# Stick-breaking mixers: which engine makes the weights' low parts and products, and where the values are evacuated

## The chip, the cores and the metric

One core of a Trainium2 chip runs the whole program in one launch. The metric is device microseconds for one execution, the median of the timed runs. Five engines run queues of their own in order: TensorE (PE; its weight loads are shown apart, as PEld), VectorE (DVE), ScalarE (ACT), GpSimd (POOL), and SP, which issues the DMAs. They are tied by semaphores.

## The reference, cut to what matters

The model is one block of dilated attention, SSM and convolution, and behind it two layers of a second kind. Each layer of the second kind is FFN, mixer, FFN, with RMS norms around them. Only the two mixers are touched. x has 512 tokens of 1024 channels; a mixer has 8 heads of 64 channels.

```python
proj = h @ w_in
q, k, v, gate_b, gate_c, conv_h, pool_in = jnp.split(proj, SPLIT_POINTS, axis=-1)
attn = _stick_breaking_attention(q, k, v)
conv = gate_b * causal_conv3(gate_c * conv_h)
pool = _multiscale_pool(pool_in, pool_w, pool_scale)   # trailing means minus the token
return jnp.concatenate([attn, conv, pool], axis=-1) @ w_out

# one query block of stick-breaking attention
z = q_blk @ k.T / sqrt(dh)                             # masked to keys before the query
log_keep = where(mask, log_sigmoid(-z), 0)
between = reverse_cumsum(log_keep) - log_keep
a = where(mask, exp(log_sigmoid(z) + between), 0)      # sigmoid(z) * product of later (1 - sigmoid)
out = a @ v
```

## The kernel before

**Precision and layout.** Channels lie on the partitions (tiles of 128 x 512 tokens). Every product of float32 matrices is made of three passes of rounded numbers: each operand is kept as a high part (ScalarE's cast) and a low part (raw minus high), and `mm3` (lines 111 to 113) multiplies high by high, low by high and high by low.

**Weights.** `Weights.prepare` (line 309 makes the low part) takes the next 512 KB of weights that a DMA has brought, lets ScalarE cast the high part `wh` and another engine subtract the low part `wl`: VectorE when no engine is named, POOL for `prepare(nc.gpsimd)`. Three raw buffers and four pairs of parts rotate.

**A mixer** (`mixer2`) runs over eight heads, n = 0 to 7, and fills TensorE's time between a head's steps with projections ("units"), by the table `FILL`: a unit is 24 matmuls of 512 columns into a bank, then an evacuation on VectorE. The names are q and k (queries and keys of a pair of heads), p (pooling input), m (pooling map, only three matmuls), g, c, l (the three parts of the convolution). Heads 0, 2, 6 and 7 have one long unit, the others two. For head n:

- `scores`: eight matmuls into three PSUM banks z; VectorE adds the mask (line 1670).
- the head before: `turn` transposes its weights (ten matmuls, line 612) into three banks, `rest` takes the low part `tl` on VectorE (line 628); `flush` splits queries into high and low parts (lines 572, 573).
- `weights`: ScalarE makes sigmoid(z) (`pr`) and sigmoid(-z) (`keep`); VectorE scans `keep` along the keys, four scans (line 1686); three products `pr` times shifted `keep` follow on POOL (line 1689).
- the first unit begins, `prepare` runs on POOL, 18 of its 24 matmuls run, then `values` of the head before: eight matmuls into the only bank `av`, and behind them the evacuation at once: ScalarE copies one half (`o`, line 1705), VectorE adds the other (line 1706), ScalarE casts the high part `oh`, VectorE subtracts the low part `ol` (line 103), on the 64 partitions of that head.
- the unit ends; at odd n the key unit's result is scaled on VectorE (`qk`, line 1855) and split at once: ScalarE copies k (lines 581, 583), VectorE makes `kl` (line 582). The scores of head n + 1 need these copies.
- further units of `FILL[n]`, a second `prepare` on POOL, and at some heads the pooling windows and means on POOL (lines 1777 to 1792).

The queues follow the order of this code (a manual schedule): nothing overtakes.

What is quoted below is printed by a program with the line numbers of the profile.

Of the kernel before, what the change touches and what calls it, by code (L numbers as in the profile page):

```python
# [10 lines left out]
ALU = mybir.AluOpType  # L11
AX = mybir.AxisListType

P = 128
# [526 lines left out]
QPLACE = [(1, 384), (2, 0), (1, 0), (0, 0)]  # L541
# [349 lines left out]
class Ssm:  # L891
# [162 lines left out]
    def collect(self, h):  # L1054

        y = self.k.gt("y", F32)
        self.k.nc.vector.scalar_tensor_tensor(y[:, :].rearrange("p (t j) -> p j t", j=L), self.u[h][:, ::-1],
                                              self.vec["dskip"][:, h:h + 1], self.yp.pop(h), ALU.mult, ALU.add)
        self.y.append(y)
# [586 lines left out]
class StickHead(Head):  # L1646
# [25 lines left out]
    def weights(self):  # L1672
        k, nc, zs = self.k, self.k.nc, self.zs
        self.pr, keep = [], []
        for b in range(3):
            w = WIDTH[b]
            p, e = k.gt("pr", F32), k.gt("keep", F32)
            nc.scalar.activation(e[:, :w], zs[b][:, :w], AF.Sigmoid, scale=-1.0)
            nc.scalar.activation(p[:, :w], zs[b][:, :w], AF.Sigmoid)
            self.pr.append(p)  # L1680
            keep.append(e)
        for qb in (3, 2, 0, 1):
            b, c = QPLACE[qb]
            e = keep[b][:, c:c + (qb + 1) * P][:, ::-1]
            zero = k.zero[:, 0:1].to_broadcast([P, (qb + 1) * P])
            nc.vector.tensor_tensor_scan(e, e, zero, 1.0, ALU.mult, ALU.add)  # L1686
        for b in range(3):
            n = WIDTH[b] - 1
            nc.gpsimd.tensor_tensor(self.pr[b][:, :n], self.pr[b][:, :n], keep[b][:, 1:n + 1], ALU.mult)

    def values(self):

        k, rows = self.k, self.rows
        c, n = divmod(self.h, 2)
        cols = slice(c * P, (c + 1) * P)
        av = k.pav.tile([P, S], F32, tag="av", name=k.uid("av"))
        for kb in range(4):
            b, c = KPLACE[kb]
            cs = slice(c, c + S - kb * P)
            for x in (self.th[b], self.tl[b]):  # L1700
                k.nc.tensor.matmul(av[:, kb * P:S], self.v[kb][n][:, cols], x[:, cs],
                                   start=kb == 0 and x is self.th[b], stop=kb == 3 and x is self.tl[b],
                                   skip_group_check=True)
        o = k.tmp("o")
        k.nc.scalar.copy(o[rows], av[self.other])
        k.nc.vector.tensor_tensor(o[rows], av[rows], o[rows], ALU.add)
        k.split(self.oh[rows], self.ol[rows], o[rows])


class Channel:  # L1710
# [23 lines left out]
class ShortConv:  # L1734
# [10 lines left out]
    def do_conv(self, ps):  # L1745
        k, nc, y, cw = self.k, self.k.nc, self.gc, self.cw
        hh = k.tmp("hh")
        nc.vector.tensor_tensor(hh, ps, self.st.R, ALU.mult)
        nc.vector.tensor_tensor(hh, y, hh, ALU.mult)
        nc.scalar.activation(y, hh, AF.Copy, scale=cw(2))  # L1750
        nc.vector.scalar_tensor_tensor(y[:, 1:], hh[:, :S - 1], cw(1), y[:, 1:], ALU.mult, ALU.add)
        nc.vector.scalar_tensor_tensor(y[:, 2:], hh[:, :S - 2], cw(0), y[:, 2:], ALU.mult, ALU.add)
        nc.gpsimd.tensor_tensor(y, y, self.st.R, ALU.mult)

    def do_last(self, ps):
        k = self.k
# [86 lines left out]
def mixer2(k, l, X, st, first, vec, gpost, gnext, start):  # L1843
    nc = k.nc
# [14 lines left out]
    def flush():  # L1859
        while later:  # L1860
            later.pop(0)()
# [4 lines left out]
    def unit(name):  # L1866
        kind, i = name[0], int(name[1])
        if kind in "qk":
            return query_key(i, "qk".index(kind))
        return {"p": lambda: pool[i].input, "m": lambda: pool[i].map, "g": lambda: conv[i].gate,  # L1870
                "c": lambda: conv[i].conv, "l": lambda: conv[i].last}[kind]()
# [11 lines left out]
    flush()  # L1883
    v += [first.end(tt) for tt in range(2, 4)]
    unit("p0").whole()
    prev = None
    for n in range(8):
        if n % 2 == 0:
            slot(n // 2)
        head = StickHead(k, n, qk[n // 2], v, (oh[n // 2], ol[n // 2]))  # L1890
        head.scores()
        if prev:
            prev.turn()
            prev.rest()
            flush()
        head.weights()
        u = unit(FILL[n][0])
        u.begin(False)
        k.w.prepare(nc.gpsimd)
        u.run(0, 6)  # L1900
        if prev:
            prev.values()
        u.run(6, KT)
        u.end()
        if n % 2:
            flush()
        for name in FILL[n][1:]:
            u = unit(name)
            u.begin(False)
            u.run(0, len(u.hi))  # L1910
            u.end()
        k.w.prepare(nc.gpsimd)
        if n % 2 == 0 and n < 4:
            pool[n // 2].windows()
        if n == 0 or n == 3:
            pool[n // 2].mean()
        if n == 1:
            pool[0].prepare()
        if n == 4:
            pool[1].prepare()  # L1920
        prev = head
# [6 lines left out]
    last.end()  # L1928
    flush()
    prev.values()  # L1930


    post = PostNorm(k, X, gpost, gnext)
# [143 lines left out]
```

## Time and profile before

| | us |
|---|---|
| median of three timed runs | 2549.23 |
| lowest and highest | 2548.54, 2550.1 |
| the profiled execution | 2553.54 |
| its span, first to last instruction | 2551.8 |
| TensorE busy in it | 2476.5 |
| VectorE busy | 1262.1 |
| ScalarE busy | 997.5 |
| POOL busy | 586.5 |

The profiled execution is one execution under the profiler, and times of single instructions come from it. A matmul's record is longer than its share of TensorE's time, since matmuls are pipelined: 512 columns stand at 0.39 us, and the next starts about 0.23 us later. "Idle before" an instruction is time in which its engine did nothing, and the arrow names what ended it. An engine's instruction that is blocked inside the engine looks like a long instruction, not like a wait. The first mixer's heads lie between 1046 and 1167 us of the span, the second's between 2002 and 2123.

### The profile page before, as it was taken

The page shows a single profiled execution, that of the slowest core. Times are in us where ns is not written, and L with a number is a line of the kernel's source. Part 1 is how long each engine was busy: PE and PEld are TensorE (multiplying, and loading weights), DVE is VectorE, ACT ScalarE, POOL GpSimd, SP SyncE. Part 2 cuts the span into 40 slices and gives each one's busy share as a digit, 9 for nine tenths or more (in the row PEclk, how much of TensorE's full clock was granted, in tenths as well). Part 3 has the DMA queues.
Part 4 walks back from the last instruction along what each step waited for, and adds up shares of the span by engine and source line. Part 5 has one row for each costly group of instructions (what it writes and reads, how often), then busy time and mean ns, then how long its engine had stood idle before and what let it go on. Part 6 is the DMA issues. An engine that isn't in the chain of part 4 may idle for free.

```text
span 2551.8 us, 30104 instructions
## 1 busy us (share of the span) xinstructions
PE 2476.5 (97%) x11792; PEld 2052.8 (80%) x11792; DVE 1262.1 (49%) x1848; ACT 997.5 (39%) x1576; POOL 586.5 (23%) x556
## 2 busy tenths in 40 slices
PE   8898999999999999999999999999999999999998
PEld 4687888888888888778788888888888778788887
DVE  6657575543534424774633423533424874643422
ACT  3356444332433323654433223433323654433322
POOL 7213220001211102473311101211102473311101
PEclk9999999999999999999999999999999999999999
DMA  6333444332233232212233232233332212223232
GB/s 247 103 123 112 151 155 156 117 99 91 91 99 98 89 96 81 68 59 91 84 98 99 87 100 87 91 99 99 92 92 81 68 59 91 90 92 99 87 102 68
DMA packets 87697, 254.80 MB, mean 100 GB/s; under 512 B 13698, under 2 KB 19842, under 8 KB 87556
## 3 DMA queue, kind: packets, MB, share of 16 engines
q1 hardware_dynamic: 86980, 252.35, 31.1%
q8 instruction: 93, 1.52, 0.2%
q10 hardware_dynamic: 576, 0.52, 0.1%
q14 instruction: 48, 0.39, 0.0%
HBM read 249.56 MB, written 3.39 MB: 99 GB/s over the span
## 4 chain that ended last, share of the span: by engine, by line
PE 80%; DVE 11%; ACT 3%; POOL 2%; issue 2%; DMA 1%; SPq 0%; DVEq 0%; ACTq 0%; POOLq 0%
PE mm L111 25%; PE mm L113 25%; PE mm L112 25%; DVE keep L1686 2%; PE mm L344 2%; DVE wa L507 1%; DVE acc L441 1%; POOL x L1587 1%; DVE fs L1579 1%; DVE x L1587 1%; DVE xl L107 1%; DVE q L573 1%; DMA wa<-wada 1%; PE n L372 1%; DVE tl L628 1%
## 5 line engine op out<-in xcount | busy, mean ns | idle before, releaser
L309 DVE TENSOR_TENSOR wl<-wr,wh 128x1024 fp32r<-128x1024 f32 (+2 forms) x383 | 448.7, 1176 | 936.0 <-ACT wh L308 935.7
L308 ACT CAST wh<-wr 128x1024 fp32r<-128x1024 f32 (+3 forms) x444 | 430.7, 979 | 549.9 <-PE mm L112 510.0
L111 PE MATMUL mm<-xh,wh 128*128 128x512 f32 x1568 | 616.4, 393 | 0.4
L113 PE MATMUL mm<-xh,wl 128*128 128x512 f32 x1568 | 611.5, 390 | 0.0
L112 PE MATMUL mm<-xl,wh 128*128 128x512 f32 x1568 | 611.4, 390 | 0.0
L111 PEld LDWEIGHTS mm<-xh,wh 128*128 128x128 f32 x1568 | 295.3, 188 | 62.5 <-DVE ol L107 1.4
L113 PEld LDWEIGHTS mm<-xh,wl 128*128 128x128 f32 x1568 | 295.0, 188 | 62.3 <-DVE wl L309 0.5
L111 PE MATMUL mm<-gh,wh 128*128 128x512 f32 (+1 forms) x936 | 343.7, 367 | 0.0
L112 PEld LDWEIGHTS mm<-xl,wh 128*128 128x128 f32 x1568 | 295.3, 188 | 60.1
L113 PE MATMUL mm<-gh,wl 128*128 128x512 f32 (+1 forms) x936 | 342.0, 365 | 0.0
L112 PE MATMUL mm<-gl,wh 128*128 128x512 f32 (+1 forms) x936 | 342.0, 365 | 0.0
L1631 POOL TENSOR_TENSOR ff<-ff,R 128x512 f32<-128x512 f32 x88 | 113.7, 1293 | 789.8 <-ACT ff L1630 789.8
L441 POOL TENSOR_TENSOR acc<-acc,sq 128x512 f32<-128x512 f32 (+1 forms) x85 | 93.9, 1104 | 717.3 <-ACT sq L428 716.4
L112 PEld LDWEIGHTS mm<-gl,wh 128*128 128x128 f32 x936 | 176.5, 189 | 28.8
L111 PEld LDWEIGHTS mm<-gh,wh 128*128 128x128 f32 x936 | 176.5, 189 | 28.8
L113 PEld LDWEIGHTS mm<-gh,wl 128*128 128x128 f32 x936 | 176.5, 189 | 28.2
L309 POOL TENSOR_TENSOR wl<-wr,wh 128x1024 fp32r<-128x1024 f32 (+2 forms) x61 | 135.3, 2227 | 243.7 <-ACT wh L308 242.7
L111 PE MATMUL mm<-uh,wh 128*128 128x512 f32 x424 | 170.5, 402 | 6.7 <-DVE vl L103 6.7
L112 PE MATMUL mm<-ul,wh 128*128 128x512 f32 x424 | 166.3, 392 | 0.0
L113 PE MATMUL mm<-uh,wl 128*128 128x512 f32 x424 | 166.2, 392 | 0.0
L102 ACT CAST gh<-ff 128x512 fp32r<-128x512 f32 x88 | 54.7, 621 | 171.1 <-DVE ff L1633 171.1
L1630 ACT ACTIVATE ff<-ff 128x512 f32<-128x512 f32 x88 | 55.6, 632 | 155.9 <-DVE ff L1629 155.8
(350 smaller groups left out, 3258.7 us busy)
## 6 DMA issues: line engine op xcount, KB each, us to landing
wr<-wg SPq DMA_DIRECT2D x88, 512.0 KB, 3.5
wr<-wu SPq DMA_DIRECT2D x88, 512.0 KB, 3.5
wr<-wd SPq DMA_DIRECT2D x80, 512.0 KB, 3.5
wr<-wi SPq DMA_DIRECT2D x56, 512.0 KB, 3.5
wa<-wada SPq DMA_DIRECT2D x64, 256.0 KB, 4.6
wr<-wup SPq DMA_DIRECT2D x32, 512.0 KB, 3.5
wr<-wo SPq DMA_DIRECT2D x24, 512.0 KB, 3.5
wr<-wd SPq DMA_DIRECT2D x32, 384.0 KB, 3.1
```

The source lines that it names most:

```text
L102: self.nc.scalar.copy(hi, raw)
L111: mm(out, wh, xh, start=start, stop=False, **kw)
L112: mm(out, wh, xl, start=False, stop=False, **kw)
L113: mm(out, wl, xh, start=False, stop=stop, **kw)
L308: self.k.nc.scalar.copy(hi[:, a:b], raw[:, a:b])
L309: e.tensor_tensor(lo[:, a:b], raw[:, a:b], hi[:, a:b].bitcast(F32), ALU.subtract)
L344: mm = lambda ps, w, x, a, b: k.nc.tensor.matmul(ps[:, cs], w, x, start=a, stop=b, skip_group_check=True)
L441: engine.tensor_tensor(self.acc[:, c0:c1], self.acc[:, c0:c1], sq[:, c0:c1], ALU.add)
L1587: engine.tensor_tensor(x, x, self.f[i][:, cs], ALU.add)
L1630: nc.scalar.activation(t, t, AF.Silu)
L1631: nc.gpsimd.tensor_tensor(t, t, st.R, ALU.mult)
L1686: nc.vector.tensor_tensor_scan(e, e, zero, 1.0, ALU.mult, ALU.add)
```

## The change

Four things are edited. The low parts of the weights at both places of a head, and the three products of the weights and the convolution's last product (`gc`), are issued on VectorE instead of POOL; each product stands right behind the scans of its bank. `values` ends with its matmuls; the new `collect` evacuates them, and is called behind `flush`, so behind the key's scaling and its copies. Copy and sum of a head still work on its 64 partitions, but both heads of a pair write into one tile `o`, and the split into `oh` and `ol` is made once for the pair, at the odd head, over 128 partitions.

```diff
--- before.py
+++ after.py
@@ -1679,14 +1679,14 @@
             nc.scalar.activation(p[:, :w], zs[b][:, :w], AF.Sigmoid)
             self.pr.append(p)
             keep.append(e)
-        for qb in (3, 2, 0, 1):
-            b, c = QPLACE[qb]
-            e = keep[b][:, c:c + (qb + 1) * P][:, ::-1]
-            zero = k.zero[:, 0:1].to_broadcast([P, (qb + 1) * P])
-            nc.vector.tensor_tensor_scan(e, e, zero, 1.0, ALU.mult, ALU.add)
-        for b in range(3):
+        for b, qbs in enumerate(((3,), (2, 0), (1,))):
+            for qb in qbs:
+                c = QPLACE[qb][1]
+                e = keep[b][:, c:c + (qb + 1) * P][:, ::-1]
+                zero = k.zero[:, 0:1].to_broadcast([P, (qb + 1) * P])
+                nc.vector.tensor_tensor_scan(e, e, zero, 1.0, ALU.mult, ALU.add)
             n = WIDTH[b] - 1
-            nc.gpsimd.tensor_tensor(self.pr[b][:, :n], self.pr[b][:, :n], keep[b][:, 1:n + 1], ALU.mult)
+            nc.vector.tensor_tensor(self.pr[b][:, :n], self.pr[b][:, :n], keep[b][:, 1:n + 1], ALU.mult)
 
     def values(self):
 
@@ -1701,10 +1701,18 @@
                 k.nc.tensor.matmul(av[:, kb * P:S], self.v[kb][n][:, cols], x[:, cs],
                                    start=kb == 0 and x is self.th[b], stop=kb == 3 and x is self.tl[b],
                                    skip_group_check=True)
-        o = k.tmp("o")
+        self.av = av
+
+    def collect(self, pair):
+
+        k, rows, av = self.k, self.rows, self.av
+        if not pair:
+            pair.append(k.tmp("o"))
+        o = pair[0]
         k.nc.scalar.copy(o[rows], av[self.other])
         k.nc.vector.tensor_tensor(o[rows], av[rows], o[rows], ALU.add)
-        k.split(self.oh[rows], self.ol[rows], o[rows])
+        if self.h % 2:
+            k.split(self.oh, self.ol, pair.pop())
 
 
 class Channel:
@@ -1750,7 +1758,7 @@
         nc.scalar.activation(y, hh, AF.Copy, scale=cw(2))
         nc.vector.scalar_tensor_tensor(y[:, 1:], hh[:, :S - 1], cw(1), y[:, 1:], ALU.mult, ALU.add)
         nc.vector.scalar_tensor_tensor(y[:, 2:], hh[:, :S - 2], cw(0), y[:, 2:], ALU.mult, ALU.add)
-        nc.gpsimd.tensor_tensor(y, y, self.st.R, ALU.mult)
+        nc.vector.tensor_tensor(y, y, self.st.R, ALU.mult)
 
     def do_last(self, ps):
         k = self.k
@@ -1883,7 +1891,7 @@
     flush()
     v += [first.end(tt) for tt in range(2, 4)]
     unit("p0").whole()
-    prev = None
+    prev, pair = None, []
     for n in range(8):
         if n % 2 == 0:
             slot(n // 2)
@@ -1896,7 +1904,7 @@
         head.weights()
         u = unit(FILL[n][0])
         u.begin(False)
-        k.w.prepare(nc.gpsimd)
+        k.w.prepare()
         u.run(0, 6)
         if prev:
             prev.values()
@@ -1904,12 +1912,14 @@
         u.end()
         if n % 2:
             flush()
+        if prev:
+            prev.collect(pair)
         for name in FILL[n][1:]:
             u = unit(name)
             u.begin(False)
             u.run(0, len(u.hi))
             u.end()
-        k.w.prepare(nc.gpsimd)
+        k.w.prepare()
         if n % 2 == 0 and n < 4:
             pool[n // 2].windows()
         if n == 0 or n == 3:
@@ -1928,6 +1938,7 @@
     last.end()
     flush()
     prev.values()
+    prev.collect(pair)
 
 
     post = PostNorm(k, X, gpost, gnext)
```

On POOL at the begin of the first mixer, before (`pr`: products of the weights; `wl`: low parts of weights; `s`, `d`: pooling windows and means):

```order
L1689 TENSOR_TENSOR pr_8170<-pr_8170,keep_8171 128x511
L1689 TENSOR_TENSOR pr_8174<-pr_8174,keep_8175 128x511
L1689 TENSOR_TENSOR pr_8178<-pr_8178,keep_8179 128x255
L309 TENSOR_TENSOR wl_8191<-wr_8059,wh_8190 128x1024
L309 TENSOR_TENSOR wl_8223<-wr_8065,wh_8222 128x128
L1777 COPY s_8228<-p_8152 128x1
L1778 TENSOR_TENSOR s_8228<-p_8152 128x511
L1786 COPY d_8231<-s_8228 64x512
L1787 COPY d_8231<-s_8228 64x2
L1788 TENSOR_TENSOR d_8231<-s_8228 64x510
```

and the same place with the change:

```order
L1785 COPY s_8228<-p_8152 128x1
L1786 TENSOR_TENSOR s_8228<-p_8152 128x511
L1794 COPY d_8231<-s_8228 64x512
L1795 COPY d_8231<-s_8228 64x2
L1796 TENSOR_TENSOR d_8231<-s_8228 64x510
L1798 TENSOR_TENSOR d_8231<-d_8231,cst 128x16
L1799 TENSOR_SCALAR d_8231<-d_8231,cst 128x496
L1800 TENSOR_TENSOR d_8231<-d_8231,p_8152 128x512
L1785 COPY s_8505<-p_8375 128x1
L1786 TENSOR_TENSOR s_8505<-p_8375 128x511
```

Products and low parts are gone, and the pooling branch of head 0 (d_8231) and then that of head 2 (from s_8505) stand first on POOL, with nothing ahead of them.

On VectorE, from head 1's scans (`keep`) to the end of its key and value work, before (`o`, `ol`: the values of head 0; `qk`, `kl`: the key; `p`: the pooling input; `dl`: its low part; `z`: masks of head 2):

```order
L1686 SCALAR_TENSOR_TENSOR keep_8284<-keep_8284,zero 128x512
L1686 SCALAR_TENSOR_TENSOR keep_8288<-keep_8288,zero 128x384
L1686 SCALAR_TENSOR_TENSOR keep_8288<-keep_8288,zero 128x128
L1686 SCALAR_TENSOR_TENSOR keep_8292<-keep_8292,zero 128x256
L1706 TENSOR_TENSOR o_8330<-av_8321,o_8330 64x512
L103 TENSOR_TENSOR ol_8155<-o_8330,oh_8154 64x512
L1855 SCALAR_TENSOR_TENSOR qk_8341<-mm_8302,R_6943 128x512
L582 TENSOR_TENSOR kl_8345<-qk_8341,k_8343 64x512
L582 TENSOR_TENSOR kl_8345<-qk_8341,k_8344 64x512
L1770 TENSOR_TENSOR p_8377<-mm_8352,R_6943 128x512
L103 TENSOR_TENSOR dl_8386<-d_8231,dh_8385 128x512
L1670 TENSOR_TENSOR z_8391<-z_8391,cst 128x128
```

and with the change:

```order
L1687 SCALAR_TENSOR_TENSOR keep_8284<-keep_8284,zero 128x512
L1689 TENSOR_TENSOR pr_8283<-pr_8283,keep_8284 128x511
L1687 SCALAR_TENSOR_TENSOR keep_8288<-keep_8288,zero 128x384
L1687 SCALAR_TENSOR_TENSOR keep_8288<-keep_8288,zero 128x128
L1689 TENSOR_TENSOR pr_8287<-pr_8287,keep_8288 128x511
L1687 SCALAR_TENSOR_TENSOR keep_8292<-keep_8292,zero 128x256
L1689 TENSOR_TENSOR pr_8291<-pr_8291,keep_8292 128x255
L1863 SCALAR_TENSOR_TENSOR qk_8336<-mm_8302,R_6943 128x512
L582 TENSOR_TENSOR kl_8340<-qk_8336,k_8338 64x512
L582 TENSOR_TENSOR kl_8340<-qk_8336,k_8339 64x512
L1713 TENSOR_TENSOR o_8347<-av_8321,o_8347 64x512
L1778 TENSOR_TENSOR p_8375<-mm_8350,R_6943 128x512
```

The three products have come between the scans; the key's scaling and low parts have moved ahead of the values' sum; the values' low part is gone here, since head 0 is the first of its pair; a low part of weights follows behind the pooling input.

## Rows read from the trace of the kernel before

**Rows 1.** The page's chain of waits: share of the span by engine

```profile
PE 80%; DVE 11%; ACT 3%; POOL 2%; issue 2%; DMA 1%; SPq 0%; DVEq 0%; ACTq 0%; POOLq 0%
```

**Rows 2.** Windows of both mixers: stretch, length, busy us (count) by engine, clock

```profile
1046.30:1167.00 120.70, 111.13 (x529) 90.56 (x528) 99.72 (x135) 71.16 (x130) 81.86 (x61) 0.97 0.19 62
2002.30:2123.00 120.70, 111.11 (x529) 90.56 (x528) 99.61 (x135) 71.19 (x131) 81.80 (x61) 0.97 0.20 62
```

**Rows 3.** What TensorE waited for, first mixer: total us, times, longest

```profile
PE z L1661 <- ACT k L583: 6.3, 3, 2.4
PE mm L612 <- POOL pr L1689: 1.5, 4, 0.7
```

**Rows 4.** Window after the longest key wait, columns as in rows 2

```profile
1102.10:1109.00 6.90, 6.90 (x23) 5.85 (x23) 5.14 (x9) 5.00 (x11) 5.22 (x5) 0.51 0.28 89
```

**Rows 5.** VectorE's groups, first mixer: busy us, mean ns | idle before

```profile
L1686 DVE TENSOR_TENSOR_SCAN keep<-keep,zero 128x512 f32<-128x512 f32 (+3 forms) x32 | 34.7, 1144 | 0.2
L573 DVE TENSOR_TENSOR q<-qk,q 64x512 fp32r<-64x512 f32 x6 | 8.0, 1331 | 0.2
L103 DVE TENSOR_TENSOR ol<-o,oh 64x512 fp32r<-64x512 f32 x7 | 7.2, 1034 | 5.0 <-ACT oh L102 5.0
L582 DVE TENSOR_TENSOR kl<-qk,k 64x512 fp32r<-64x512 f32 x6 | 4.9, 818 | 3.3 <-ACT k L581 3.2
L103 DVE TENSOR_TENSOR dl<-d,dh 128x512 fp32r<-128x512 f32 x2 | 3.2, 1586 | 0.8 <-ACT dh L102 0.8
L1749 DVE TENSOR_TENSOR hh<-gc,hh 128x512 f32<-128x512 f32 x2 | 2.8, 1424 | 0.1
```

**Rows 6.** VectorE's groups by form, same stretch: the 384-column scan

```profile
L1686 DVE TENSOR_TENSOR_SCAN keep<-keep,zero 128x384 f32<-128x384 f32 x8 | 7.4, 928 | 0.0
```

**Rows 7.** Timeline: POOL, then VectorE's scans: start, us, idle before

```profile
1061.78 1.04 POOL L1788 TENSOR_TENSOR d<-s 64x510 f32<-64x510 f32 x1
...
1065.31 1.29 POOL L1792 TENSOR_TENSOR d<-d,p 128x512 f32<-128x512 f32 x1
1061.80 5.35 DVE L1686 TENSOR_TENSOR_SCAN keep<-keep,zero 128x512 f32<-128x512 f32 x4
```

**Rows 8.** VectorE's groups by form, whole span: prices

```profile
L309 DVE TENSOR_TENSOR wl<-wr,wh 128x1024 fp32r<-128x1024 f32 x319 | 393.2, 1238 | 808.5 <-ACT wh L308 808.3
L103 DVE TENSOR_TENSOR gl<-ff,gh 128x512 fp32r<-128x512 f32 x88 | 61.0, 693 | 60.5 <-ACT gh L102 60.5
...
L628 DVE TENSOR_TENSOR tl<-mm,th 128x256 fp32r<-128x256 f32 x8 | 3.3, 415 | 0.0
```

**Rows 9.** POOL's groups, first mixer, columns as in rows 5

```profile
L309 POOL TENSOR_TENSOR wl<-wr,wh 128x1024 fp32r<-128x1024 f32 (+1 forms) x15 | 34.7, 2325 | 9.9 <-ACT wh L308 9.9
L1689 POOL TENSOR_TENSOR pr<-pr,keep 128x511 f32<-128x511 f32 (+1 forms) x24 | 27.5, 1162 | 35.2 <-DVE keep L1686 35.2
L1753 POOL TENSOR_TENSOR gc<-gc,R 128x512 f32<-128x512 f32 x2 | 2.9, 1456 | 8.8 <-DVE gc L1752 8.8
```

**Rows 10.** VectorE's waits for ScalarE, first mixer, columns as in rows 3

```profile
DVE ol L103 <- ACT oh L102: 5.0, 7, 0.8
DVE kl L582 <- ACT k L581: 3.2, 5, 0.8
DVE gc L1751 <- ACT gc L1750: 1.6, 2, 0.8
DVE o L1706 <- ACT o L1705: 1.6, 2, 1.1
```

**Rows 11.** Timeline at head 1's end: VectorE, then TensorE

```profile
1067.07 0.65 DVE L1706 TENSOR_TENSOR o<-av,o 64x512 f32<-64x512 f32 x1
1069.55 0.67 DVE L1855 SCALAR_TENSOR_TENSOR qk<-mm,R 128x512 f32<-128x512 f32 x1
1071.57 0.91 PE L1661 MATMUL z<-k,q 128*128 128x512 f32 x4 [1.81 <-ACT k L583]
```

**Rows 12.** Window of head 2, columns as in rows 2

```profile
1071.50:1081.50 10.00, 9.93 (x52) 8.44 (x53) 8.55 (x13) 8.30 (x16) 3.46 (x2) 1.00 0.18 54
```


## The prediction

> **What bounds the kernel now.** The chain of waits first: four fifths of the span are TensorE's own matmuls and most of the rest is VectorE [rows 1]. The change touches only the two mixers, so I then read each mixer as one stretch, from the first score matmul to the last values matmul. They are alike: 120.7 us each, VectorE busy for 99.7 us, POOL for 81.9, the granted clock 0.97 on average [rows 2]. TensorE waits there mostly for the keys' copies (6.3 us in three waits, the longest 2.4) and for the product of the weights, which POOL makes (1.5 us) [rows 3]. After the longest of the key waits the clock falls to half (1.2 of 2.4 GHz), 0.51 over 6.9 us [rows 4], which costs about 3.4 us of matmuls. So 11 us of each stretch are TensorE's losses, and VectorE, though not the engine that is fullest, stands in front of nearly all of them. The reader is to see that VectorE's 99.7 us are not all work. A scan of 384 columns takes 0.93 us [rows 6]; the four scans of a head have 1280 columns together, so 3.1 us by the same price, 24.7 us for eight heads, and they took 34.7 [rows 5]. The timeline shows why: beside four POOL instructions that ran one after the other from 1061.78 to 1066.60, the four scans took 5.35 us, and their ends take turns with POOL's [rows 7]. VectorE's instructions with two SBUF operands stand still while a POOL instruction runs.
>
> The Trainium skill says so too (SBUF — State Buffer, section "SBUF: two separate sides"): the pair of ports that VectorE and GpSimd share is locked for a whole instruction and the other engine blocks fully. The trace agrees in kind; how much of POOL's record that is, the rows decide below.
>
> **The change, part by part, for one mixer.** All is summed on VectorE's own time, because after the change it is the engine with the most work that waits for others.
>
> What goes away with POOL's work is the blocking. Against the free price of 0.69 us for 512 columns [rows 8] the groups with two SBUF operands lose: scans 34.7 − 24.7 = 10.0; the query splits 8.0 − 6 × 0.69 = 3.9; the values' low parts 7.2 − 7 × 0.69 = 2.4; the keys' low parts 4.9 − 4.1 = 0.8; the pooling branch's low parts 3.2 − 1.4 = 1.8; the convolution's product 2.8 − 1.4 = 1.4 [rows 5]. Together 20.3 us. VectorE's work as such is 99.7 − 20.3 = 79.4 us.
>
> What comes to VectorE: 24 products of the weights, 16 of 511 columns at 0.69 us and 8 of 255 columns at 0.42 [rows 8], 14.4 us (POOL took 27.5 for them [rows 9]). Fifteen low parts of weights (34.7 us on POOL [rows 9]): thirteen of 128x1024 at 1.24 us [rows 8] less 0.08, because records that follow each other overlap (32 scans of 1.144 cover 34.7 and not 36.6 [rows 5]), 15.1 us, and two of 128x128, at most 0.4 each, 0.8. Two products of the convolution, 1.4 us (2.9 on POOL [rows 9]). The values' low parts are halved, since one instruction over 128 partitions takes as long as one over 64: seven in the stretch become three, −2.8 us. Sum +28.9 us, so 108.3 us.
>
> The GPSIMD Engine Reference of the Trainium skill (section 4.1, "Engine selection") speaks for this part: elementwise work belongs on VectorE, GPSIMD being about twice as slow with two inputs. The rows agree (1.24 against 2.33 us for the weights). By that rule alone the change is a gain; what it would give is the first rival.
>
> What is left of the blocking: POOL keeps the pooling windows and means, 81.9 − 34.7 − 27.5 − 2.9 = 16.8 us [rows 2, 9]. Before, they stood on POOL behind products and low parts; now nothing stands ahead of them, so they start as soon as their input is evacuated, and in heads 0 and 2 they meet the scans and products on VectorE. The bounds are 0 (all of it falls on VectorE's idle time or beside its PSUM readers) and 16.8 (one for one). In the row that is nearest, four scans lost 5.35 − 3.1 = 2.3 us to 4.8 us of POOL [rows 7], which is half, so I take 8.4 us: 116.7.
>
> What is left of VectorE's waits: it answers ScalarE inside one queue, and these replies stay. Keys 3.2, convolution 1.6, values' copy 1.6, and the values' hi part, 5.0 for seven, now 2.1 for three [rows 10]: 8.5 us. Nothing else is queued on VectorE that could run meanwhile. The wait for the transposed weights (th) I leave out, since VectorE will come late there. 116.7 + 8.5 = 125.2 us, against 120.7 now: +4.5 us a mixer, +9.0 for both.
>
> The keys' evacuation is a gain of place, and it is in the sum already. In head 1 the values' sum began at 1067.07 and the key's scaling only at 1069.55, after which TensorE waited 1.81 us for the key [rows 11]. Now the key's scaling stands right behind the third product, and 2.48 us come before it no more, but three products (1.8 us) do: 0.7 us earlier by order, and some 2 us more because the scans are not blocked. So the key waits shrink or go, and with them the drop of the clock. What is late next is the transposes. Each needs the products of the head before and a PSUM bank that VectorE must evacuate behind two low parts of weights. It is worst in the short heads, where TensorE has only one long accumulation: in the stretch of head 2 VectorE is busy 8.55 of 10.0 us already [rows 12], and it gets 1.8 us of products and two low parts of 1.2 us more, against some 3 us that are freed or hidden. So I expect idle time of 2 to 5 us in front of the transposes of heads 0 and 2 and of the last heads, and with idle time in such clusters a clock at half there too. While VectorE sets the pace, a slow clock costs little.
>
> Queues: POOL issues no DMA, and the loads on SP wait for the raw buffers, which are freed when a low part is done; these are done sooner or as soon. ScalarE loses 4 copies of 0.6 us a mixer, hidden. The last values of a mixer are evacuated as before, and the code behind it is the same: 0.
>
> **Which time it is compared with.** The sum was made inside a profiled execution of 2553.54 us (span 2551.8). The three timed runs have a median of 2549.23; I put the difference on that: 2549.2 + 9.0 = 2558.2 us.
>
> **The rivals.** (1) *Faster: VectorE keeps up.* POOL's windows and means fall beside VectorE's idle time and readers of PSUM and block nothing. Then the sum is 108.3 + 8.5 = 116.8 us, −3.9 a mixer, 2541.4 us. For it: the key waits (6.3 us) and the half clock (3.4 us) are the largest losses, and the change goes at just these. Against it: both pooling branches now run exactly beside scans and products. It decides from 3.9 us of blocking a mixer on: below that the kernel is faster than before. (2) *No difference*: blocking of 2 to 6 us; what the keys give, the transposes take: 2545 to 2554 us. (3) *Worse: POOL blocks for its whole record*, 16.8 us: 133.6 us, +12.9 a mixer, 2575 us. For it: a VectorE instruction and a POOL instruction take turns one for one in the rows, and the chain has seven links instead of four. Against it: POOL's records contain its own waiting for the lock. The rule of the Trainium skill on the locked pair (SBUF — State Buffer, "SBUF: two separate sides"), taken at its word, gives this end. (4) *The later evacuation holds the only bank of the values* until the next head's values want it: a wait of under 1 us in one or two heads, inside the range.
>
> **How the numbers follow.** About 0.2% (5 us) can be told from no change. My forecast, VectorE bound with some half of the blocking, 2554.5 to 2568 us: 0.52. Rival 3, above 2568: 0.09. Rival 2: 0.22. Rival 1, below 2544: 0.17. So slower 0.61, same 0.22, faster 0.17. The range of 8 in 10 is 2542 to 2568: it leaves out about 0.1 at each end, and corresponds to 0.3 to 13 us of blocking a mixer.
>
> **What would show it.** Right: VectorE over 95% of the stretch in use or waiting for ScalarE, its scans at 0.4 to 1.25 us outside heads 0 and 2, POOL's windows beside the first head's scans, TensorE's waits for keys down from 6.3 to under 2 us, and new waits of transposes and of their banks for VectorE of over 10 us a mixer, the stretch 122 to 130 us long. Wrong: key waits gone and no new ones for the transposes (rival 1); scans of head 0 over 10 us with their products (rival 3); or a stretch outside the mixers that has changed, which my sum says cannot be.

## The result and the profile after

The changed kernel takes 2564.6 us (median of four runs, 2560.58 to 2566.98) where the kernel before takes 2549.55 on the same chip: a ratio of 1.0057, 95% interval 1.0041 to 1.0073. It is slower by some 15 us. The profiled execution took 2566.98 us, its span is 2565.2 us, 13.4 more than before. The page's chain of waits has moved by one point from TensorE to VectorE [rows 1]:

```profile
PE 79%; DVE 12%; ACT 3%; POOL 2%; issue 2%; DMA 1%; SPq 0%; DVEq 0%; ACTq 0%; POOLq 0%
```

The windows of both mixers, columns as in [rows 2], from the first score matmul to the last values matmul:

```profile
1046.70:1173.90 127.20, 113.08 (x529) 92.19 (x528) 112.62 (x172) 68.27 (x126) 18.15 (x20) 0.95 0.19 62
2008.85:2136.40 127.55, 113.45 (x529) 91.81 (x528) 112.45 (x172) 68.20 (x126) 18.20 (x20) 0.95 0.19 61
```

Between their exact ends the two stretches are 6.5 and 6.9 us longer than before (from 120.5 us each to 127.1 and 127.4), and together that is the whole difference of the spans: nothing outside the mixers has moved. POOL is down from 82 to 18 us, VectorE up from 99.7 to 112.6. What TensorE waited for in the first mixer, columns as in [rows 3]:

```profile
PE mm L612 <- DVE pr L1689: 4.5, 4, 1.9
PE mm L111 <- DVE ol L107: 3.9, 2, 2.3
PE mm L612 <- DVE qk L1863: 1.9, 1, 1.9
PE av L1701 <- DVE tl L628: 1.8, 2, 1.2
PE z L1661 <- ACT k L583: 1.2, 1, 1.2
PE mm L612 <- DVE hh L1756: 0.9, 1, 0.9
```

The key waits have shrunk from 6.3 to 1.2 us. In their place stand waits for VectorE: for the products, and for PSUM banks that VectorE evacuates (`ol` at line 107 is the evacuation of the pooling map, `qk` that of the queries, `hh` that of a part of the convolution). VectorE's groups of the same stretch, columns as in [rows 5]:

```profile
L1687 DVE TENSOR_TENSOR_SCAN keep<-keep,zero 128x512 f32<-128x512 f32 (+3 forms) x32 | 27.9, 892 | 0.2
L309 DVE TENSOR_TENSOR wl<-wr,wh 128x1024 fp32r<-128x1024 f32 (+1 forms) x16 | 18.7, 1167 | 0.6 <-ACT wh L308 0.5
L1689 DVE TENSOR_TENSOR pr<-pr,keep 128x511 f32<-128x511 f32 (+1 forms) x24 | 17.0, 707 | 2.5
L573 DVE TENSOR_TENSOR q<-qk,q 64x512 fp32r<-64x512 f32 x6 | 4.1, 686 | 0.2
L103 DVE TENSOR_TENSOR ol<-o,oh 128x512 fp32r<-128x512 f32 x3 | 2.1, 693 | 2.1 <-ACT oh L102 2.1
```

Scans fell from 34.7 to 27.9 us and the query splits from 8.0 to 4.1: the blocking by POOL is mostly gone, as computed. But 17.0 us of products and 18.7 us of low parts have come, and in front of the products VectorE is idle for 2.5 us with no other engine named. The timeline of head 0 on VectorE shows what that is (start, us, instruction, count):

```profile
1051.41 1.46 DVE L1687 TENSOR_TENSOR_SCAN keep<-keep,zero 128x512 f32<-128x512 f32 x1
1052.97 0.85 DVE L1689 TENSOR_TENSOR pr<-pr,keep 128x511 f32<-128x511 f32 x1
1053.74 2.06 DVE L1687 TENSOR_TENSOR_SCAN keep<-keep,zero 128x384 f32<-128x384 f32 x2
1055.90 1.12 DVE L1689 TENSOR_TENSOR pr<-pr,keep 128x511 f32<-128x511 f32 x1
1056.94 1.75 DVE L1687 TENSOR_TENSOR_SCAN keep<-keep,zero 128x256 f32<-128x256 f32 x1
1058.79 0.42 DVE L1689 TENSOR_TENSOR pr<-pr,keep 128x255 f32<-128x255 f32 x1
```

The first scan ends at 1052.87 and the product that reads it starts at 1052.97, 0.10 us later; the scan behind, which depends on nothing new, starts at 1053.74, 0.08 us before the product's record ends. The chain lasts 7.8 us here, beside POOL's windows. At the transposes of head 2, which stand in head 3, TensorE shows what follows from VectorE being late (in brackets the idle time before):

```profile
1086.57 0.88 PE L612 MATMUL mm<-cst,pr 128*128 128x128 f32 x6 [0.38 <-DVE pr L1689]
1089.38 0.55 PE L612 MATMUL mm<-cst,pr 128*128 128x128 f32 x3 [1.94 <-DVE qk L1863]
1092.27 0.79 PE L111 MATMUL mm<-xh,wh 128*128 128x512 f32 x1 [2.34 <-DVE ol L107]
```

In the last of these waits the granted clock falls to half (1.2 of 2.4 GHz). The window, columns as in [rows 2]:

```profile
1090.20:1097.00 6.80, 4.74 (x11) 3.77 (x12) 6.12 (x11) 6.75 (x14) 0.00 (x0) 0.50 0.40 142
```

It does so at 1059.4 and 1141.4 too, for 3.4 us each. Together 13.6 us of the first mixer are at half, against 6.8 before [rows 4].

Head by head (from a head's first score matmul to the next head's, in the trace; first mixer, us):

| head | 0 | 1 | 2 | 3 | 4 | 5 | 6 | 7 |
|---|---|---|---|---|---|---|---|---|
| before | 7.1 | 18.1 | 10.3 | 19.4 | 18.2 | 17.2 | 10.3 | 19.9 |
| after | 7.1 | 20.3 | 10.2 | 22.5 | 14.9 | 17.4 | 11.9 | 22.9 |

Heads 1, 3 and 7, in which the transposes of heads 0, 2, 6 and 7 stand, are longer by 2 to 3 us each, head 6 by 1.6; head 4, in which the half clock behind the longest key wait lay [rows 4], is shorter by 3.3.

### The profile page after: what moved, and what is told of

It is laid out like the page before. It is cut to its first block, busy times and chain, and to the rows that moved or that the text cites. A ratio compares the mean times of both kernels' runs of the same rounds, so it can differ in the third digit from the quotient of the medians.

```text
span 2565.2 us, 30060 instructions
## 1 busy us (share of the span) xinstructions
PE 2482.5 (97%) x11792; PEld 2058.3 (80%) x11792; DVE 1285.4 (50%) x1922; ACT 991.4 (39%) x1568; POOL 456.2 (18%) x474
## 4 chain that ended last, share of the span: by engine, by line
PE 79%; DVE 12%; ACT 3%; POOL 2%; issue 2%; DMA 1%; SPq 0%; DVEq 0%; ACTq 0%; POOLq 0%
PE mm L111 25%; PE mm L113 25%; PE mm L112 25%; DVE keep L1687 2%; PE mm L344 2%; DVE wl L309 1%; DVE wa L507 1%; DVE pr L1689 1%; POOL x L1587 1%; DVE fs L1579 1%; DVE x L1587 1%; DVE acc L441 1%; DVE xl L107 1%; DMA wa<-wada 1%; DVE tl L628 1%
## 5 line engine op out<-in xcount | busy, mean ns | idle before, releaser
L309 DVE TENSOR_TENSOR wl<-wr,wh 128x1024 fp32r<-128x1024 f32 (+3 forms) x413 | 483.5, 1175 | 937.8 <-ACT wh L308 937.3
L309 POOL TENSOR_TENSOR wl<-wr,wh 128x1024 fp32r<-128x1024 f32 (+1 forms) x31 | 66.2, 2140 | 222.8 <-ACT wh L308 221.8
```

The lines of the kernel that those rows point to most:

```text
L309: e.tensor_tensor(lo[:, a:b], raw[:, a:b], hi[:, a:b].bitcast(F32), ALU.subtract)
```

## The experiments

**Theory A**, that of the prediction: VectorE's queue (own work, blocking by POOL, replies to ScalarE) sets the pace of the changed kernel, and the new waits come from it. The rivals: **B**, the late evacuation costs; **C**, POOL blocks VectorE for its whole record, and this is the loss; **D**, only the half clock matters; **E**, POOL blocks nothing. F to I belong to single runs below. All ratios are against the kernel before, run on the same chip.

**The evacuation alone.** Products, low parts and the convolution's product are back on POOL, and the scans in their old order; values behind the keys and split by pair. Against the kernel before:

```diff
+        self.av = av
+
+    def collect(self, pair):
...
-        k.split(self.oh[rows], self.ol[rows], o[rows])
+        if self.h % 2:
+            k.split(self.oh, self.ol, pair.pop())
...
         if n % 2:
             flush()
+        if prev:
+            prev.collect(pair)
```

> The kernel before with only the evacuation changed: values behind the keys', split by pair; products and low parts stay on POOL. Theory A (the loss is VectorE's longer queue, and the evacuation by itself is a gain): VectorE loses four low parts of values a mixer (4 x 1.03 = 4.1 us) and three waits for their high parts (5.0 to 2.1 us), and the key waits of 6.3 us shrink to under 3 us; with them the half clock behind them (3.4 us) goes: the stretch falls from 120.7 to 112 to 117 us, 2532 to 2542 us. Theory B (the late evacuation costs, by holding the only bank of the values): slower than before, 2552 us or more. Theory D (only the half clock matters): 2543 us, 3.4 us a mixer.

Measured: 2535.96 us, ratio 0.9945 (0.9933 to 0.9957). The windows:

```profile
1042.80:1156.00 113.20, 107.99 (x529) 89.39 (x529) 98.49 (x131) 68.16 (x126) 80.16 (x61) 0.98 0.20 66
1991.40:2104.60 113.20, 107.98 (x528) 89.34 (x528) 95.19 (x131) 68.15 (x126) 80.78 (x61) 0.98 0.20 66
```

The stretch is 113.0 us, 7.5 less than before. TensorE's waits in it:

```profile
PE mm L111 <- DVE ol L107: 3.2, 2, 2.5
PE mm L612 <- POOL pr L1689: 1.7, 4, 0.7
```

No key wait is left that the row shows; the half clock is down to 3.4 us a mixer, behind the wait of 2.5. So this part of the change is a gain of 14 us, and B falls. It holds two things, the later place and the split by pair, and no run has the one without the other. Of D's 3.4 us a mixer the run gives twice as much, so D alone is too small. The rest of the change must then cost some 29 us.

**Low parts back on POOL.** The changed kernel with

```diff
-        k.w.prepare()
+        k.w.prepare(nc.gpsimd)
```

at both places of a head.

> The changed kernel, with the low parts of the weights back on POOL; products on VectorE, evacuation late. Theory A (VectorE's own work sets the pace, POOL's records are half lost on it): 18.7 us of low parts leave VectorE and 34.7 us of POOL come back, half of them 17.4 us: nothing is won, the stretch stays within 3 us of 127.2, 2559 to 2571 us. Theory C (a POOL instruction blocks VectorE for its whole record): 34.7 - 18.7 = 16 us a mixer worse where VectorE cannot hide it, 2580 us or more. Theory E (the work on VectorE alone counts, POOL's blocking is nothing): 18.7 us of VectorE's work less, the stretch at most 115 us, 2540 us or less.

Measured: 2570.54 us, ratio 1.0072 (1.0060 to 1.0085), stretches of 129.4 and 129.1 us. VectorE's groups:

```profile
L1687 DVE TENSOR_TENSOR_SCAN keep<-keep,zero 128x512 f32<-128x512 f32 (+3 forms) x32 | 36.2, 1150 | 0.2
L1689 DVE TENSOR_TENSOR pr<-pr,keep 128x511 f32<-128x511 f32 (+1 forms) x24 | 21.6, 902 | 2.5
```

17.5 us of VectorE's own work are gone, and the scans have 8.3 us more and the products 4.6 us more than in the changed kernel, because now the low parts on POOL block them. VectorE is busy for 114.3 us, more than with the low parts. So nothing is won, as A had it. E, which wanted under 2540, falls, and so does C's 2580.

**Products back on POOL**, behind all four scans:

```diff
-        for b, qbs in enumerate(((3,), (2, 0), (1,))):
+        for qb in (3, 2, 0, 1):
...
-            nc.vector.tensor_tensor(self.pr[b][:, :n], self.pr[b][:, :n], keep[b][:, 1:n + 1], ALU.mult)
+            nc.gpsimd.tensor_tensor(self.pr[b][:, :n], self.pr[b][:, :n], keep[b][:, 1:n + 1], ALU.mult)
```

> The changed kernel, with the three products of the weights back on POOL behind all four scans; low parts of weights on VectorE, evacuation late. Theory A: 17.0 us of products leave VectorE, with 2.5 us in which they waited for their own scans; POOL gets 27.5 us, half lost on VectorE, 13.8 us at most, and less where they run beside VectorE's readers of PSUM: the stretch falls by 3 to 8 us to 119 to 124, 2548 to 2559 us. Theory C (whole records): 27.5 - 19.5 = 8 us worse, 2580 us. Theory E (no blocking): 19.5 us less of VectorE, TensorE is then the bound, under 115 us, 2540 us or less.

Measured: 2547.56 us, ratio 0.9986 (0.9977 to 0.9995):

```profile
1045.20:1163.40 118.20, 109.65 (x529) 89.19 (x528) 106.45 (x148) 68.36 (x127) 49.01 (x44) 0.99 0.20 66
1998.80:2114.20 115.40, 108.44 (x528) 87.94 (x528) 104.54 (x148) 68.32 (x126) 52.29 (x44) 1.00 0.21 68
```

Stretches of 118.0 and 115.3 us. C is far off. In time the run lies at the lower edge of A's range (2548 us) and 7 us from E's 2540; in the stretch, 116.7 us on average, it lies between A's 119 and E's 115. So A took too much of POOL's blocking here, and this run alone does not exclude E; the run before and the next one do. The low parts (with the convolution's product) cost 3.6 us a mixer against the evacuation alone; the products, with their place between the scans, cost more than I had given them.

**No pooling windows.** The changed kernel without them, POOL empty in the mixers:

```diff
-        if n % 2 == 0 and n < 4:
-            pool[n // 2].windows()
         if n == 0 or n == 3:
-            pool[n // 2].mean()
+            pool[n // 2].d = pool[n // 2].p
```

> The changed kernel without the pooling windows and means: POOL does nothing in the mixers, the pooling map gets the pooling input itself (that part of the computation is left out). It measures what these 18 us of POOL cost VectorE. Theory A as predicted (half of 16.8 us, 8.4 us a mixer): the stretch falls from 127.2 to 118.8, the time from 2564.6 to 2548 us. By the excess of VectorE's own records in the changed kernel (scans 3.2, products 2.6, one low part 1.1): 7 us, 2551 us. Theory C (whole records): 16.8 us a mixer, 2531 us. Theory E (no blocking): 2564 us.

Measured: 2553.07 us, ratio 1.0005 (0.9996 to 1.0013); by the ratios 0.52% or 13 us less than the changed kernel. The windows and VectorE's groups:

```profile
1045.50:1166.60 121.10, 110.06 (x529) 89.07 (x528) 106.53 (x172) 68.21 (x126) 0.00 (x0) 0.99 0.20 65
2001.90:2123.70 121.80, 112.08 (x528) 90.99 (x528) 106.32 (x172) 68.14 (x126) 0.00 (x0) 0.96 0.20 65
```

```profile
L1687 DVE TENSOR_TENSOR_SCAN keep<-keep,zero 128x512 f32<-128x512 f32 (+3 forms) x32 | 25.3, 812 | 0.2
L1689 DVE TENSOR_TENSOR pr<-pr,keep 128x511 f32<-128x511 f32 (+1 forms) x24 | 14.5, 603 | 2.5
```

VectorE loses 6.1 us of busy time and the stretches (120.9 and 121.7) 5.9 on average: this is what POOL's 18.2 us cost, between E (nothing) and C (all of it). And with no POOL at all, the stretch is still 8 us longer than with the evacuation alone: more than half of what the moved work costs is VectorE's own queue.

**The evacuation undone**, the rest of the change kept:

```diff
-        self.av = av
...
+        o = k.tmp("o")
         k.nc.scalar.copy(o[rows], av[self.other])
         k.nc.vector.tensor_tensor(o[rows], av[rows], o[rows], ALU.add)
-        if self.h % 2:
-            k.split(self.oh, self.ol, pair.pop())
+        k.split(self.oh[rows], self.ol[rows], o[rows])
...
-        if prev:
-            prev.collect(pair)
```

> The changed kernel with the evacuation undone: low parts, products and the convolution's product on VectorE, the values evacuated at once and split by head, as before. Theory A (VectorE's queue sets the pace in this kernel, so what leaves it is paid in full): the evacuation saved VectorE four low parts (4 x 0.69 = 2.8 us) and 2.9 us of waits for the values' high parts a mixer, so without it the stretch grows by 4 to 7 us to 131 to 134, the time to 2574 to 2581 us. Theory F (the gain of the late evacuation was the keys only, and these no longer bound TensorE here): no difference to the changed kernel, 2562 to 2570 us. If its two halves simply add, the stretch grows by the 7.5 us that the evacuation alone gave: 2581 us.

Measured: 2577.81 us, ratio 1.0098 (1.0084 to 1.0112), stretches of 131.8 and 132.4. TensorE's waits:

```profile
PE mm L612 <- DVE pr L1689: 5.3, 4, 1.9
PE z L1661 <- ACT k L583: 3.9, 2, 3.2
PE mm L612 <- DVE qk L1855: 3.4, 1, 3.4
```

The key waits are back (3.9 us). The evacuation is worth 4.9 us a mixer here, as A had it (4 to 7), less than the 7.5 alone. Theory F falls: the work moved to VectorE does not make the evacuation idle.

**The order of scans and products.** The changed kernel with its products on VectorE, but behind all four scans (the loop of the product run above, with `nc.vector`).

> The changed kernel with its three products on VectorE behind all four scans, in the order of before (3, 2, 0, 1), instead of each behind the scans of its bank. Theory G (the interleaved order costs, because each product waits in the queue for the scan just ahead of it: 2.5 us of idle time in front of the products a mixer): the stretch falls by 1.5 to 2.5 us, the time to 2561 to 2564 us on a chip where the changed kernel takes 2566. Rival (the earlier first product lets the transposes begin earlier, which is worth more): slower by 1 to 3 us a mixer, 2568 to 2572 us.

Measured: 2556.46 us, ratio 1.0016 (1.0007 to 1.0025): 10 us less than the changed kernel by the ratios, stretches of 122.9 and 121.9. The sign is that of G, the size is twice what I had given. VectorE's groups:

```profile
L1686 DVE TENSOR_TENSOR_SCAN keep<-keep,zero 128x512 f32<-128x512 f32 (+3 forms) x32 | 25.9, 869 | 0.2
L1689 DVE TENSOR_TENSOR pr<-pr,keep 128x511 f32<-128x511 f32 (+1 forms) x24 | 13.2, 601 | 0.0
L1863 DVE SCALAR_TENSOR_TENSOR qk<-mm,R 128x512 f32<-128x512 f32 x6 | 4.1, 680 | 1.5 <-PE mm L113 1.5
```

The 2.5 us of idle time in front of the products are gone, and their records are 3.8 us shorter, those of the scans 2.0. VectorE now even waits for TensorE at times (1.5 us before `qk`, 3.6 us in all).

Was that VectorE's pipeline, or POOL that got in between a scan and its product? The same kernel **without the pooling windows**, edited as above:

> The changed kernel with its products on VectorE behind all four scans, and without the pooling windows and means (that part of the computation is left out): what the order of scans and products costs where POOL does nothing. Theory H (the order costs by VectorE's own pipeline: a product that reads the scan just ahead starts after its end, while independent instructions overlap by 0.08 us; 2.5 us of waits and about 1.3 us of overlap a mixer): 3.8 us less than the 121.3 us of the kernel without windows, 117.5 us a mixer, some 2545 us where that kernel takes 2553. Theory I (the order costs only because POOL gets in between scan and product): no difference, 2553 us.

Measured: 2541.53 us, ratio 0.9968 (0.9956 to 0.9981), stretches of 115.8 us. The window and VectorE's groups:

```profile
1046.10:1162.00 115.90, 109.31 (x528) 89.08 (x527) 103.73 (x172) 68.22 (x126) 0.00 (x0) 0.99 0.21 67
```

```profile
L1686 DVE TENSOR_TENSOR_SCAN keep<-keep,zero 128x512 f32<-128x512 f32 (+3 forms) x32 | 23.7, 803 | 0.2
L1689 DVE TENSOR_TENSOR pr<-pr,keep 128x511 f32<-128x511 f32 (+1 forms) x24 | 12.8, 588 | 0.0
```

Without POOL the order costs 5.5 us a mixer, with it 4.8. So it is not POOL (I falls); it is the dependence between neighbours in one queue, as H says, though larger than H's 3.8: 2.5 us of waits, and 2.8 us of VectorE's busy time (106.5 against 103.7 us), since its records overlap less. It is not the change from one kind of instruction to the other: behind the four scans the first product, which reads the first of them, starts before the last scan's end (1055.92 against 1055.99 us in head 0 of the run with POOL's windows). At 24 places a mixer, 0.10 us of gap and 0.08 us of overlap that is lost make 4.4 us (an estimate); H had put the overlap at 1.3 us.

**Two refinements of the evacuation alone.** In its run TensorE waited 2.46 us behind the transposes of head 2 for the pooling map's bank; VectorE had the pair's low part ahead of that evacuation, and it took 2.36 us beside a low part of weights on POOL. First, the split behind the later units of each head:

```diff
         k.nc.vector.tensor_tensor(o[rows], av[rows], o[rows], ALU.add)
-        if self.h % 2:
-            k.split(self.oh, self.ol, pair.pop())
...
             u.end()
+        if prev and prev.h % 2:
+            k.split(prev.oh, prev.ol, pair.pop())
         k.w.prepare(nc.gpsimd)
```

> The evacuation alone (products and low parts on POOL), and in addition the pair's split stands behind the later units of the head, so behind the evacuation of the pooling map. In the run of the evacuation alone TensorE waited 2.46 us at head 2's end and 0.72 us at head 6's for a bank whose evacuation stood on VectorE behind the pair's low part, which took 2.36 us beside a low part of weights on POOL. Theory A (VectorE's queue sets what waits are left): both waits go, with the half clock behind the first (0.8 us more): 3 to 4 us a mixer less, 2528 to 2531 us on a chip where the evacuation alone takes 2536. Rival (the blocked low part only moves, and now stands ahead of the next head's scans): 2535 to 2538 us.

Measured: 2536.51 us, ratio 0.9938 (0.9926 to 0.9951), stretches of 111.9 us. The stretch lost 1.1 us, not 3 to 4, and the times cannot be told from those of the evacuation alone: the rival had it right. The two waits and the half clock are gone, but others came: 1.4 us for a key and 1.5 us for a bank of the convolution.

Then, in addition, the second low part of heads 1 and 2 on VectorE:

```diff
-        k.w.prepare(nc.gpsimd)
+        k.w.prepare(None if n in (1, 2) else nc.gpsimd)
```

> As the split behind the later units, and in heads 1 and 2 the second low part of weights is made on VectorE instead of POOL: two instructions of 1.24 us that come to VectorE a mixer, two of 2.4 us that leave POOL just ahead of the blocked split and the scans. Theory A (what counts is VectorE's queue at that place, own work and blocking together): 2.5 us of own work against at most 4.8 us of blocking, half of it lost: no difference to the split behind the later units within 2 us a mixer. If blocking counts in full: 2.3 us a mixer faster, 5 us in all.

Measured: 2532.81 us, ratio 0.9924 (0.9912 to 0.9937), stretches of 110.5 us, 1.4 less than the run before. That lies within the 2 us that A allowed, but is nearer to the 2.3 us of blocking in full than to no difference; the run does not decide between them. TensorE waits 3.6 us a mixer and its clock is full throughout. The wait of 1.26 us for the convolution's bank at 1098.86 remains; VectorE's timeline ahead of it:

```profile
1094.02 0.68 DVE L582 TENSOR_TENSOR kl<-qk,k 64x512 fp32r<-64x512 f32 x1 [0.81 <-ACT k L581]
1095.23 2.26 DVE L582 TENSOR_TENSOR kl<-qk,k 64x512 fp32r<-64x512 f32 x1 [0.53 <-ACT k L581]
1097.53 0.68 DVE L1713 TENSOR_TENSOR o<-av,o 64x512 f32<-64x512 f32 x1
1098.13 0.67 DVE L1749 TENSOR_TENSOR gc<-mm,R 128x512 f32<-128x512 f32 x1
```

The same instruction takes 0.68 us free and 2.26 us beside a low part of weights that POOL began at 1094.07. Whether the moved split or this key's low part is behind that wait, the last run tells: the split moved in head 2 alone.

```diff
...
-        if prev and prev.h % 2:
+        if n == 2:
             k.split(prev.oh, prev.ol, pair.pop())
```

> The evacuation behind the keys with products and low parts on POOL, the pair's split behind the later unit in head 2 alone, and the second low part of heads 1 and 2 on VectorE. In the run with the split behind the later units in all heads, heads 4 took 16.6 us, where with the split ahead they took 14.9. If that was the moved split: 1.7 us a mixer less, 2529 us on a chip where that kernel takes 2533. If it comes from head 3's key (its low part stood 2.26 us beside a low part of weights on POOL, and the convolution's bank came free late behind it): the split of head 4 has no part in it, no difference, 2532 to 2534 us.

Measured: 2532.82 us, ratio 0.9931 (0.9918 to 0.9945), stretches of 111.1; TensorE's waits:

```profile
PE mm L111 <- DVE gc L1751: 1.5, 2, 1.3
PE z L1661 <- ACT k L583: 1.3, 2, 0.7
```

The wait for `gc` is the same: the moved split has no part in it. The version with the split behind all later units and two low parts on VectorE beats both kernels of this document, by 0.76% the one before and by 1.3% the changed one; most of that is the evacuation alone.

The mixers of the kernels that build up the change (stretches of the two mixers between their exact ends; VectorE's busy time of both, averaged; half clock: us at 1.2 GHz in both mixers together, from the granted clock):

| kernel | ratio | stretches, us | VectorE busy | half clock |
|---|---|---|---|---|
| before | 1 | 120.5, 120.5 | 99.7 | 14 |
| evacuation alone | 0.9945 | 113.0, 113.1 | 96.8 | 7 |
| + low parts on VectorE | 0.9986 | 118.0, 115.3 | 105.5 | 3 |
| + products on VectorE, scans first | 1.0016 | 122.9, 121.9 | 108.3 | 24 |
| + products between the scans = changed | 1.0057 | 127.1, 127.4 | 112.5 | 27 |

The stretches come from one profiled execution each. By the ratios of the timed runs the four steps are −7.0, +5.2, +3.8 and +5.2 us a mixer, each uncertain by some 2 us. So the gain of the evacuation, the cost of both moves together and that of the order are clear of the noise; how the cost of the moves divides between low parts and products is not.

## Why the prediction was right, and where it was not

The forecast was 2558.2 us, slower by 9; it is slower by 15, inside the range. The lines above split the +6.7 us a mixer into single edits: the evacuation −7.5, the low parts and the convolution's product +3.6, the products on VectorE +5.7, their place between the scans +4.8.

*What bounds the kernel, and that the loss goes to VectorE's queue: right.* VectorE is busy for 112.6 and waits for ScalarE for 10.4 of 127.2 us, 97%. The key waits fell to 1.2 us, the new waits for VectorE sum to 13 us (transposes and their banks 7.3, banks of units 3.9, the low parts `tl` 1.8; the prediction wanted over 10 us of the first kind alone, and that sign was missed), the stretch is inside 122 to 130, the idle time and the half clocks stand where they were forecast (transposes of heads 0 and 2, the last heads), and nothing changed outside the mixers.

*VectorE's own work: right to 2 us.* 108.3 forecast; with POOL empty it is 106.5 in the changed order and 103.7 with the scans first. The price of the products (14.4) was met (14.5).

*What is left of the blocking: 8.4 forecast, 5.9 measured* (no pooling windows), within the bounds 0 and 16.8. So rival 3 was wrong, and rival 1 missed its own condition, under 3.9. By the blocking alone rival 2 (2 to 6 us, no difference) would have come true; the next term is why it did not.

One instruction of VectorE does stand beside a whole one of POOL (2.26 against 0.68 us above), and still 18.2 us of POOL's records cost only 5.9. Part of them, so it seems, is POOL's own waiting: the same window sum took 1.04 us in [rows 7] and, in the changed kernel's head 0 (timeline),

```profile
1053.82 1.70 POOL L1796 TENSOR_TENSOR d<-s 64x510 f32<-64x510 f32 x1
```

The Trainium skill (SBUF — State Buffer, "SBUF: two separate sides") has the shared pair of ports locked for a whole instruction and the other engine fully blocked. Summed over POOL's records, as rival 3 took it, that would be 17 to 18 us a mixer; the run gave a third of it, and the measurement decides: a rule for one instruction does not price a stretch.

*VectorE's waits: 8.5 forecast, 14.6 idle measured.* This is the term that was mis-sized. What VectorE waited for in the first mixer, columns as in [rows 3]:

```profile
DVE kl L582 <- ACT k L581: 3.9, 6, 0.7
DVE ol L103 <- ACT oh L102: 2.1, 3, 0.7
DVE o L1713 <- ACT o L1712: 1.7, 3, 0.6
DVE gc L1759 <- ACT gc L1758: 1.6, 2, 0.8
DVE v L107 <- ACT v L106: 1.1, 2, 0.5
DVE hh L1756 <- PE mm L113: 0.9, 1, 0.9
```

The replies to ScalarE were 10.4 instead of 8.5; the `v` of 1.1 us was not on the list. The larger part was left out: 1.4 us of waits for TensorE and the weights' cast, and 2.5 us in which a product waits for the scan just ahead of it. I had subtracted 0.08 us of overlap per record for the low parts and never asked whether scan and product overlap in the new order; they do not, and the two pairs of runs that differ in this alone price gap and lost overlap at 4.8 to 5.5 us a mixer. The chain of seven links, which the prediction named only as an argument for rival 3, was the point.

*The evacuation: about right in this kernel, too small by itself.* "A gain of place, and it is in the sum already" gave it 2.8 us of low parts and 2.9 of waits, 5.7 a mixer. Where VectorE is the limit that is about right: 4.9. Alone it is 7.5; there TensorE's key waits (6.3 us) and half of its half clock go as well, which would explain it but was not tested by itself. With the measured terms the sum is 106.5 + 5.9 + 14.6 = 127.0 us for a stretch of 127.1; the forecast had 108.3 + 8.4 + 8.5 = 125.2, two terms too high by 4.3 us and one too low by 6.1. The measured sum closes because it is busy time plus idle time; that the forecast came within 2 us of it is in part luck, since its errors offset each other.

*"While VectorE sets the pace, a slow clock costs little"* is borne out in part. TensorE's busy time is 113.1 us in the changed kernel and 107.1 in the version with two low parts on VectorE, whose clock was never at half, so some 6 us of its stretch are slow matmuls. What they cost, the two mixers of one execution show. Without the pooling windows these spent 3.4 and 10.2 us at half clock, with VectorE equally busy (windows above), and the second stretch is only 0.8 us longer; with the low parts on POOL it was 23.9 and 13.7 us, and the stretches are 129.4 and 129.1; with the scans first 13.7 and 10.2 us, and 122.9 and 121.9. If all of it counted, the more at half clock would have cost 3.4, 5.1 and 1.7 us (an estimate from these times); it cost at most 0.8, 0.3 and 0.9. But no run set the clock alone. In the step that moves the products the half clock rises from 3 to 24 us, VectorE's busy time by only 2.8 us a mixer, and its waits for TensorE from 0.5 to 3.6: how much of that step is VectorE's queue and how much the clock stays open.

Moved to VectorE, low parts and products cost 9 us a mixer even with the better order: TensorE waits for VectorE's queue, and had rarely waited for POOL's [rows 3]. The Trainium skill (GPSIMD Engine Reference, section 4.1) puts elementwise work on VectorE. By the price of one instruction the rows agree: 1.24 us [rows 8] against 2.58 for the same 128x1024 on POOL. The 2.33 that the prediction set beside 1.24 is a mean with two short ones [rows 9]; POOL's group by form, before:

```profile
L309 POOL TENSOR_TENSOR wl<-wr,wh 128x1024 fp32r<-128x1024 f32 x13 | 33.4, 2577 | 9.9 <-ACT wh L308 9.9
```

By the time of the kernel the rows do not agree.

## What to carry to other kernels

Price a move by the queue it goes into: POOL at 2.58 us an instruction was cheaper than VectorE at 1.24, because VectorE stood in front of TensorE's next matmul and POOL did not. Put the evacuation that TensorE's next step needs first, and the one that nobody waits for behind it: together with the split by pair that gave 0.55% by itself, and the other edits hid it. In one queue, keep a dependent instruction away from its producer where an independent one can stand between.

## What the runs showed of the hardware

Two VectorE instructions that follow each other overlap by about 0.08 us in their records; a product that reads the scan just ahead starts 0.10 us after its end, and in the convolution a `hh` that reads the `hh` just ahead starts 0.03 us after it. With 24 such pairs a mixer, the order alone was worth 5 us of 120, about as much as all that POOL still took from VectorE. POOL's 18.2 us of records cost the stretch 5.9 us in the changed kernel, and 20.0 us cost 6.6 with the scans first (122.4 against 115.8 us): about a third, whichever the order.
